# The MLP as a second phase over all tokens, each matrix product in seven half-size ones (Strassen)

## The chip, the cores and the metric

The kernel runs on one core of a Trainium2 chip. The metric is device time in microseconds of one launch. Five engines work side by side, each through its own list of instructions in order: TensorE (PE, with its weight loads as PEld), VectorE (DVE), ScalarE (ACT), GpSimd (POOL), and SyncE (SP), which issues nearly all of the DMAs here. An instruction whose input is not there yet holds up everything behind it on its engine.

## The reference

One layer of a decoder with two kinds of mixer heads: 2048 prompt tokens and 8 x 4 sample tokens, 1024 features, all in fp32.

```python
h = rmsnorm(x, g_mix); proj = h @ w_in              # 1024 x 4624
# RG-LRU: conv, gates, linear recurrence, gelu gate, norm      -> y_lru (1024)
# SSD: conv, silu, 16 heads in chunks of 128, silu gate, norm  -> y_ssd (1024)
x = x + jnp.concatenate([y_lru, y_ssd], axis=-1) @ w_out       # 2048 x 1024
m = rmsnorm(x, g_mlp)
x = x + jnp.square(jax.nn.relu(m @ w_up)) @ w_down             # 1024 x 4096, 4096 x 1024
y = rmsnorm(x, g_final)
```

The states of convolutions and recurrences are outputs too.

## The kernel before

Features lie on the partitions, tokens in the columns. The 2080 tokens are done in three parts of 768, 672 and 640 columns (PARTS), each in two blocks of at most 384 (a PSUM bank): 384 + 384, 384 + 288, 384 + 256. A part runs through all stages before the next one begins: x_phase (load, norm, transpose), dt and group fronts, eight pairs of SSD heads (pair_front, pair_x, pair_mats, pair_back), eight RG-LRU tiles (lru_front, lru_back), the w_out projection in three calls of proj_add, and the MLP. Its last w_down comes after the next part's x_phase in program order; final writes the part's output rows.

An fp32 product is made of three fast ones (mm3, L217): weights and activations are each split into a rounded high half (type fp32r) and the rest, and high by high, low by high and high by low go into one bank (L225 to L227). load_w (L199) brings a weight block of eight 128x128 tiles by one DMA of SP into one of three raw buffers, ScalarE copies it to the high half (L208), and VectorE subtracts for the low half (L214); SHARE and SH1 say which of these subtractions GpSimd takes: those of one w_out call. Loads wait for a raw buffer to come free.

The MLP of a part has four groups of FFQ = 8 feature tiles. up (L787) makes a tile by 24 matmuls for each block, then relu (L800), square (L801), high half (L802) on ScalarE and the low half (L803) on VectorE; proj_add (L413) multiplies by w_down and on VectorE scales by the token's norm (L428) and adds to the residual x (X2 tiles, in SBUF, L429). The norm's square is applied only there, so that up needs no norm. final (L822) turns two tiles of 128 tokens at a time back to rows in four PSUM banks (L837), squares them (L838), takes the reciprocal root by twelve small VectorE operations (rsqrt, L233, and those around it), multiplies (L850) and stores (L853).

The order on every engine is set at build by a scheduler that works from the program's order and its own estimates of when operands are there.

## Time and profile before

| | |
|---|---|
| three runs | 3058.8, 3059.4, 3061.8 us |
| the profiled execution, span of its instructions | 3050.1 us |
| busy PE, DVE, ACT, POOL | 98, 58, 46, 6% |
| instructions PE, DVE, ACT | 19294, 3192, 2424 |
| moved by DMA | 289 MB, 95 GB/s in the mean |
| granted PE clock, mean | 0.993 |

A row of the page's groups reads: line, engine, operation, output from inputs, shapes, count, then busy time in us, mean ns of one, and the engine's idle time before it with what ended it. A window's row gives the busy time of each engine between two moments, with the count of instructions. In time order the MLPs of the three parts lie near 600 to 1040, 1700 to 2050 and 2600 to 3038 us.

### The profile page before, as it was taken

Reading aid. Unit: us, or ns where it says so; the run is one execution under the profiler, and the core shown is the slowest. Engines: PE = TensorE matmul, PEld = TensorE weight load, DVE = VectorE, ACT = ScalarE, POOL = GpSimd, SP = SyncE. Lnnn points to the kernel's source line nnn. Section 1 sums busy time; section 2 is a strip of 40 time slices with the busy share of each in tenths; the row PEclk is TensorE's granted clock in tenths of the full one; section 3 lists DMA queues with packets and bytes.
Section 4 is the critical chain, followed back from the end, with each engine's and each line's share of the span. In section 5 each row is a group of like instructions: output and inputs, shape, how many; then the busy total and the mean of one; then the engine's idle time right before and its main releaser. Section 6 shows DMA issues by size and latency. Waiting matters only on the chain.

```text
span 3050.1 us, 47623 instructions
## 1 busy us (share of the span) xinstructions
PE 2986.8 (98%) x19294; PEld 2914.2 (96%) x19294; DVE 1782.4 (58%) x3192; ACT 1405.8 (46%) x2424; POOL 169.8 (6%) x282
## 2 busy tenths in 40 slices
PE   6999999999999999999989999999999999999998
PEld 5999999999999999999989999999999999999998
DVE  6777677543333457777686433336777677434336
ACT  5543775533241524436855342343554874432333
POOL 1000121000000000001310000000000120000000
PEclk9999999999999999999999999999999999999999
DMA  5332323322222323434233222223343234222224
GB/s 154 95 123 80 98 79 113 98 62 64 64 67 63 98 94 115 143 109 122 85 112 111 73 71 76 70 74 122 112 126 98 80 104 125 84 77 71 76 77 125
DMA packets 447411, 288.85 MB, mean 95 GB/s; under 512 B 23323, under 2 KB 423887, under 8 KB 447190
## 3 DMA queue, kind: packets, MB, share of 16 engines
q1 hardware_dynamic: 446966, 285.52, 31.4%
q8 instruction: 152, 2.49, 0.3%
q0 software_dynamic: 224, 0.27, 0.1%
q14 instruction: 69, 0.57, 0.1%
HBM read 255.95 MB, written 29.79 MB: 94 GB/s over the span
## 4 chain that ended last, share of the span: by engine, by line
PE 78%; DVE 3%; ACT 1%; issue 1%; DMA 1%; DVEq 0%; SPq 0%; ACTq 0%
PE mm L225 24%; PE mm L227 24%; PE mm L226 24%; PE ax L701 1%; PE ax L697 1%; PE ax L673 1%; PE ax L687 1%; PE ax L707 0%; DVE wl L214 0%; ACT wh L208 0%; DMA xT<-xraw 0%; PE ax L613 0%; ACT yt L838 0%; PE ax L757 0%; PE nx L450 0%
## 5 line engine op out<-in xcount | busy, mean ns | idle before, releaser
L225 PE MATMUL mm<-xh,wh 128*128 128x384 f32 (+3 forms) x3696 | 1188.5, 322 | 14.8 <-ACT xh L358 12.7
L227 PE MATMUL mm<-xh,wl 128*128 128x384 f32 (+3 forms) x3696 | 1184.4, 321 | 3.1 <-DVE wl L214 3.1
L226 PE MATMUL mm<-xl,wh 128*128 128x384 f32 (+3 forms) x3696 | 1184.1, 320 | 0.6 <-DVE xl L359 0.5
L208 ACT ACTIVATE wh<-raw 128x1024 fp32r<-128x1024 f32 (+1 forms) x383 | 403.5, 1053 | 1010.3 <-PE mm L226 948.8
L225 PEld LDWEIGHTS mm<-xh,wh 128*128 128x128 f32 (+1 forms) x3696 | 692.1, 187 | 25.6 <-ACT xh L358 13.7
L227 PEld LDWEIGHTS mm<-xh,wl 128*128 128x128 f32 (+1 forms) x3696 | 692.0, 187 | 9.1 <-DVE wl L214 4.4
L226 PEld LDWEIGHTS mm<-xl,wh 128*128 128x128 f32 (+1 forms) x3696 | 692.2, 187 | 5.2 <-DVE xl L359 1.5
L214 DVE TENSOR_TENSOR wl<-raw,wh 128x1024 fp32r<-128x1024 f32 (+1 forms) x371 | 450.9, 1215 | 235.9 <-ACT wh L208 230.3
L225 PE MATMUL mm<-ah,wh 128*128 128x384 f32 (+2 forms) x1536 | 494.2, 322 | 0.0
L227 PE MATMUL mm<-ah,wl 128*128 128x384 f32 (+2 forms) x1536 | 494.0, 322 | 0.0
L226 PE MATMUL mm<-al,wh 128*128 128x384 f32 (+2 forms) x1536 | 493.7, 321 | 0.0
L428 DVE TENSOR_TENSOR mm<-mm,bc 128x384 f32<-128x384 f32 (+2 forms) x336 | 176.0, 525 | 426.8 <-PE mm L227 425.1
L225 PEld LDWEIGHTS mm<-ah,wh 128*128 128x128 f32 x1536 | 289.2, 188 | 0.3
L226 PEld LDWEIGHTS mm<-al,wh 128*128 128x128 f32 x1536 | 289.0, 188 | 0.1
L227 PEld LDWEIGHTS mm<-ah,wl 128*128 128x128 f32 x1536 | 288.9, 188 | 0.1
L803 DVE TENSOR_TENSOR al<-av,ah 128x384 fp32r<-128x384 f32 x192 | 99.7, 519 | 305.0 <-ACT ah L802 304.3
L395 DVE SCALAR_TENSOR_TENSOR u<-xe,prm,u 128x768 f32<-128x768 f32 (+2 forms) x180 | 170.2, 945 | 25.9 <-ACT u L393 23.0
L800 ACT ACTIVATE av<-mm 128x384 f32<-128x384 f32 x192 | 86.4, 450 | 199.2 <-PE mm L227 199.2
L429 DVE TENSOR_TENSOR x<-x,mm 128x384 f32<-128x384 f32 (+2 forms) x336 | 172.2, 513 | 8.7
L225 PE MATMUL mm<-nh,wh 128*128 128x384 f32 (+2 forms) x384 | 128.0, 333 | 10.9 <-DVE x L429 10.7
L226 PE MATMUL mm<-nl,wh 128*128 128x384 f32 (+2 forms) x384 | 126.1, 328 | 0.0
L227 PE MATMUL mm<-nh,wl 128*128 128x384 f32 (+2 forms) x384 | 126.0, 328 | 0.0
(266 smaller groups left out, 2891.5 us busy)
## 6 DMA issues: line engine op xcount, KB each, us to landing
raw<-in_w_in_dram SPq DMA_DIRECT2D x108, 512.0 KB
raw<-in_w_down_dram SPq DMA_DIRECT2D x104, 512.0 KB
raw<-in_w_up_dram SPq DMA_DIRECT2D x96, 512.0 KB
raw<-in_w_out_dram SPq DMA_DIRECT2D x72, 512.0 KB
m<-cum SPq DMA_DIRECT2D x32, 320.0 KB
xt<-in_x_prompt_dram SPq DMA_DIRECT2D x13, 512.0 KB
xT<-xraw SPq DMA_DIRECT2D x32, 192.0 KB
m<-cum SPq DMA_DIRECT2D x16, 384.0 KB
```

Of the source, the lines that this page charges most:

```text
L208: S.activation(h, raw, AF.Copy)
L214: e.tensor_tensor(out=lo, in0=raw, in1=h.bitcast(F32), op=ALU.subtract)
L225: T.matmul(ps[:m, :n], h[:, k, :m], xh[:, c0:c0 + n], start=k == 0, stop=False)
L226: T.matmul(ps[:m, :n], h[:, k, :m], xl[:, c0:c0 + n], start=False, stop=False)
L227: T.matmul(ps[:m, :n], lo[:, k, :m], xh[:, c0:c0 + n], start=False, stop=k == nk - 1)
L395: V.scalar_tensor_tensor(out=u[:, :W], in0=xe[:, k:k + W], scalar=pc(wn, k * nt + j), in1=u[:, :W], op0=ALU.mult, op1=ALU.add)
L428: V.tensor_mul(ps[:, :n], ps[:, :n], bc[:, c0:c0 + n])
L429: V.tensor_add(P.X2[o][:, c0:c0 + n], P.X2[o][:, c0:c0 + n], ps[:, :n])
L673: T.matmul(ps[:, c * Q:c * Q + Q], R.bk[:, (a + c) * Q:(a + c + 1) * Q], xdd[:, (a + c) * Q:(a + c + 1) * Q], start=True, stop=True)
L687: T.matmul(ps, xds[:, 1], R.bex[:NS, 512 * i:512 * i + 512], start=True, stop=True)
L800: S.activation(v[:, :n], ps[:, :n], AF.Relu)
L803: V.tensor_sub(lo[:, c0:c0 + n], v[:, :n], h[:, c0:c0 + n].bitcast(F32))
```

## The change

The MLP leaves the parts. First all three parts go through the mixer stages and w_out. After each block of w_out, residual_out writes the normalised input of the MLP (with its gain) and the residual to DRAM (mn_d, x2_d). Then all mixer pools are closed and mlp() runs over all 2080 tokens, in three groups of 2 x 348 or 2 x 346 columns.

There each product is taken as a 2 x 2 product of blocks: input features in two halves, output features in two halves, tokens in two halves. Seven products of sums of blocks take the place of eight (the Winograd form, 4 sums of weight blocks, 4 of activation blocks, 7 of results). Some results are summed in PSUM, by a second product into the same bank (start=False). The seven weight operands, with high and low halves, do not depend on the tokens: they are made once, in 64 jobs that stand between the steps of the mixers. A job has four stages (load four blocks; four sums and the high half; store the high half and subtract; store the low half), and each call of tick in the mixers puts 1.0, 1.4 or 1.6 of these stages in program order at its place. They go to DRAM; the MLP loads its weights from there as finished halves, for each token group again, by 240 DMAs of up to 512 KB. jt and jh, the jobs' tiles, have one buffer each; to make room in SBUF raw has two buffers, not three, and there are 20 slots, not 22. GpSimd's share of the low halves is gone.

up makes two columns of feature tiles by seven products of 12 matmuls, twice a group of features (eight groups); the sums, relu and squares give four tiles, from which operands() makes the seven operands in halves for down. down makes four pairs of output tiles by seven products of 6 matmuls each; sums go to u (the part that three results share) or straight to x2. final takes a tile of 128 tokens at a time.

```diff
-NW = 22
-FFQ = 8
+NW = 20
 XG = 3
 KEEP = 7
-SHARE, SH1 = 0, 1
 NK = 5
+MLP = [(0, 348), (696, 346), (1388, 346)]
+MH, FQ = 348, 4
+NTOK = SEQ + NS
+TP, TL, TO = 1.4, 1.6, 1.0
...
-        raw = room("raw", F32, 3)
+        raw = room("raw", F32, 2)
-        e = V
-        if share:
-            gwn[0] += 1
-            e = G if gwn[0] % share == 0 else V
-        e.tensor_tensor(out=lo, in0=raw, in1=h.bitcast(F32), op=ALU.subtract)
+        V.tensor_tensor(out=lo, in0=raw, in1=h.bitcast(F32), op=ALU.subtract)
...
+            if tick:
+                tick(P, TO)
...
+    def mlp():
+        mp = ctx.enter_context(tc.tile_pool(name="mp", bufs=1, reuse_waits="tile"))
+        sf = ctx.enter_context(tc.tile_pool(name="sf", bufs=3, reuse_waits="tile"))
+        ps8 = ctx.enter_context(tc.tile_pool(name="ps8", bufs=6, space=PSUM))
+        psf = ctx.enter_context(tc.tile_pool(name="psf", bufs=2, space=PSUM))
...
+        def weights(src, op, m):
+            w = mp.tile([128, 2, 512], F32R, tag="mw", name="mw", bufs=6)
+            nc.sync.dma_start(w[:, :, :m].bitcast(F32), src[:, op])
+            return w
+        def product(ps, w, ops, n, start):
+            nk = len(ops)
+            for k, (xh, xl) in enumerate(ops):
+                c = slice(128 * k, 128 * k + 128)
+                for i, (wi, x) in enumerate(((0, xh), (0, xl), (1, xh))):
+                    T.matmul(ps[:, :n], w[:, wi, c], x[:, :n], start=start and k == 0 and i == 0,
+                             stop=k == nk - 1 and i == 2, skip_group_check=not start)
+        def halves(t, n, tag, bufs):
+            h = mp.tile([128, MH], F32R, tag=tag, name=tag + "h", bufs=bufs)
+            lo = mp.tile([128, MH], F32R, tag=tag, name=tag + "l", bufs=bufs)
+            S.activation(h[:, :n], t[:, :n], AF.Copy)
+            V.tensor_sub(lo[:, :n], t[:, :n], h[:, :n].bitcast(F32))
+            return h, lo
+        def operands(b, n, tag, bufs):
+            b11, b12, b21, b22 = b
+            t1, t2, t3, t4 = (tmp(f"t{i}") for i in range(4))
+            V.tensor_sub(t1[:, :n], b12[:, :n], b11[:, :n])
+            V.tensor_sub(t2[:, :n], b22[:, :n], t1[:, :n])
+            V.tensor_sub(t3[:, :n], b22[:, :n], b12[:, :n])
+            V.tensor_sub(t4[:, :n], b21[:, :n], t2[:, :n])
+            return [halves(t, n, tag, bufs) for t in (b11, t2, t1, t3, b21, b22, t4)]
+        def front(c0, n):
...
+        def up(q, u, mh, n):
+            src = up_d[2 * q + u]
+            x, y, z, w = bank(), bank(), bank(), bank()
+            product(x, weights(src, 0, 512), mh[0], n, True)
+            p1 = tmp("p1")
+            S.activation(p1[:, :n], x[:, :n], AF.Copy)
+            product(y, weights(src, 1, 512), mh[1], n, True)
+            v = tmp("v")
+            V.tensor_add(v[:, :n], p1[:, :n], y[:, :n])
+            product(z, weights(src, 2, 512), mh[2], n, True)
+            p5 = tmp("p5")
+            S.activation(p5[:, :n], z[:, :n], AF.Copy)
+            product(w, weights(src, 3, 512), mh[3], n, True)
+            c22 = tmp("c22")
+            V.tensor_add(c22[:, :n], v[:, :n], w[:, :n])
+            V.tensor_add(c22[:, :n], c22[:, :n], p5[:, :n])
+            product(x, weights(src, 4, 512), mh[4], n, False)
+            c11 = tmp("c11")
+            S.activation(c11[:, :n], x[:, :n], AF.Relu)
+            product(z, weights(src, 5, 512), mh[5], n, False)
+            c12 = tmp("c12")
+            V.tensor_add(c12[:, :n], v[:, :n], z[:, :n])
+            product(w, weights(src, 6, 512), mh[6], n, False)
+            c21 = tmp("c21")
+            V.tensor_add(c21[:, :n], v[:, :n], w[:, :n])
+            for c in (c22, c12, c21):
+                S.activation(c[:, :n], c[:, :n], AF.Relu)
+            for c in (c11, c12, c21, c22):
+                S.activation(c[:, :n], c[:, :n], AF.Square)
+            return operands((c11, c12, c21, c22), n, "ah", 29)
+        def down(q, act, x2, us, n, steps):
+            for g in range(4):
+                if steps:
+                    steps.pop(0)()
+                src = dn_d[4 * q + g]
+                hi, lo = x2[g], x2[g + 4]
+                c11, c12, c21, c22 = hi[:, :n], hi[:, n:2 * n], lo[:, :n], lo[:, n:2 * n]
+                def add(c, ps):
+                    V.tensor_add(c, c, ps[:, :n])
+                x, y, z, w = bank(), bank(), bank(), bank()
+                ws = {}
+                def prod(i, ps, start):
+                    if i % 2 == 0:
+                        t = mp.tile([128, 2, 512], F32R, tag="mw", name="mw", bufs=6)
+                        m = min(2, 7 - i)
+                        tv = t.rearrange("p a (b c) -> p (a b c)", c=256)[:, :m * 512]
+                        nc.sync.dma_start(tv.bitcast(F32).rearrange("p (o c) -> p o c", c=512),
+                                          src[:, i:i + m].rearrange("p o h c -> p o (h c)"))
+                        ws[0] = t.rearrange("p a (b c) -> p a b c", c=256)
+                    product(ps, ws[0][:, i % 2], [a[i] for a in act], n, start)
+                u = us[g][:, :n]
+                prod(0, x, True)
+                if q == 0:
+                    S.activation(u, x[:, :n], AF.Copy)
+                else:
+                    add(u, x)
+                prod(1, y, True)
+                add(u, y)
+                prod(2, z, True)
+                add(c22, z)
+                prod(3, w, True)
+                add(c22, w)
+                prod(4, x, False)
+                add(c11, x)
+                prod(5, z, False)
+                add(c12, z)
+                prod(6, w, False)
+                add(c21, w)
+                if q == NQ - 1:
+                    for c in (c12, c21, c22):
+                        V.tensor_add(c, c, u)
+        def final(c0, n, x2):
...
+                    ps = psf.tile([128, 512], F32, tag="fx", name="fx")
...
+                        T.transpose(ps[:m, 128 * k:128 * k + 128], x2[4 * hf + k][:, o:o + m], ident)
...
+                    S.activation(yt[:m], ps[:m], AF.Square, accum_out=s2[:m, hf:hf + 1])
...
+                rsqrt(rs[:m], ss[:m], 1, sf)
...
+                    V.scalar_tensor_tensor(out=yts[hf][:m], in0=pss[hf][:m], scalar=rs[:m, 0:1],
+                                           in1=gfb[:m, 512 * hf:512 * hf + 512], op0=ALU.mult, op1=ALU.mult)
...
+        mh, steps = front(*MLP[0])
+        for f in steps:
+            f()
+        prev = None
+        for i, (c0, n) in enumerate(MLP):
+            us = [mp.tile([128, MH], F32, tag="u", name="u", bufs=4) for _ in range(4)]
+            x2 = None
+            for q in range(NQ):
+                act = [up(q, u, mh, n) for u in range(2)]
+                if prev:
+                    final(*prev)
+                    prev = None
+                if x2 is None:
+                    x2 = []
+                    for o in range(KD):
+                        t = mp.tile([128, 2 * MH], F32, tag="x2", name="x2", bufs=8)
+                        nc.sync.dma_start(t[:, :2 * n], x2_d[128 * o:128 * o + 128, c0:c0 + 2 * n])
+                        x2.append(t)
+                steps = []
+                if q == NQ - 1 and i + 1 < len(MLP):
+                    mh, steps = front(*MLP[i + 1])
+                    steps.pop(0)()
+                down(q, act, x2, us, n, steps)
+            prev = (c0, n, x2)
+        final(*prev)
...
+    def job_load(j):
+        src, ld, r0, dr_, cols, _ = jobs[j]
+        t = jt[j] = wp.tile([128, 7, 256], F32, tag="jt", name="jt", bufs=1)
+        for i, at in ((0, (0, 4)), (1, (3, 6))):
+            for k in range(2):
+                nc.sync.dma_start(t[:, at[k]].rearrange("p (k n) -> p k n", n=128),
+                                  dap(src, (r0 + dr_ * k) * ld + cols[i], [[ld, 128], [128 * ld, 2], [1, 128]]))
+    def job_sums(j):
+        t = jt[j]
+        V.tensor_add(t[:, 2], t[:, 3], t[:, 6])
+        V.tensor_sub(t[:, 3], t[:, 0], t[:, 3])
+        V.tensor_sub(t[:, 1], t[:, 2], t[:, 0])
+        V.tensor_sub(t[:, 5], t[:, 4], t[:, 1])
+        h = jh[j] = wp.tile([128, 7, 256], F32R, tag="jh", name="jh", bufs=1)
+        S.activation(h, t, AF.Copy)
+    def job_lower(j):
+        nc.sync.dma_start(jobs[j][5][:, :, 0], jh[j].bitcast(F32))
+        V.tensor_tensor(out=jt[j].bitcast(F32R), in0=jt[j], in1=jh[j].bitcast(F32), op=ALU.subtract)
+    def job_store(j):
+        nc.sync.dma_start(jobs[j][5][:, :, 1], jt[j])
+        del jt[j], jh[j]
+    stages = (job_load, job_sums, job_lower, job_store)
+    def tick(P, w):
+        clock[1] += w
+        while clock[1] >= 1 and clock[0] < 4 * len(jobs):
+            clock[1] -= 1
+            stages[clock[0] % 4](clock[0] // 4)
+            clock[0] += 1
...
             xx = pair_x(P, pr, fr[0])
+            tick(P, TP)
             nx = ahead()
+            tick(P, TP)
             if pr == 4:
                 load_x2(P)
                 proj_add(P, w_out, 8, n0, bc0)
             ms_ = pair_mats(P, R, pr)
+            tick(P, TP)
             y, acc = pair_back(P, R, pr, fr, acc, ms_, xx)
+            tick(P, TP)
...
+        def residual_out(b):
+            rstd_rows(P, rstd_sums(P, accs[b], D, EPS, [P.groups[b]]), [P.groups[b]], AF.Copy, P.bc2)
             for k, t in enumerate(P.X2):
-                split(t[:, c0:c0 + n], pc("g_m", k), mh[b][k], n)
-                accs[b] = squares(accs.get(b), t, c0, n)
...
         for b in range(lastb + 1):
-            proj_add(P, w_out, 0, nl, bcl, [b])
+            proj_add(P, w_out, 0, nl, bcl, [b], tick=tick)
+            sums(b)
             if b < lastb:
-                mlp_in(b)
-        nq = FF // 128 // FFQ
-        for q in range(nq):
-            act = up(P, q, mh, (lambda: mlp_in(lastb)) if q == 0 else None)
-            if q == 0:
-                mlp_norm()
-                carried_out(P)
-            if q < nq - 1:
-                proj_add(P, w_down, q * FFQ, act, P.bc2)
+                residual_out(b)
+        carried_out(P)
         if not P.last:
             x_phase(parts[P.i + 1])
-            proj_add(P, w_down, (nq - 1) * FFQ, act, P.bc2)
-            for g in P.groups:
-                final(P, g)
-        else:
-            for b, g in enumerate(P.groups):
-                proj_add(P, w_down, (nq - 1) * FFQ, act, P.bc2, [b])
-                final(P, g)
+        residual_out(lastb)
+    tick(P, 999)
+    mix.close()
+    mlp()
```

How the order moves at three places that matter. First VectorE, where a group of features goes from up to down. Before, in the MLP of the second part (al is the low half, x the residual, bc the norm's row):

```order
L803 TENSOR_TENSOR al<-av,ah 128x384
L214 TENSOR_TENSOR wl<-raw,wh 128x1024
L803 TENSOR_TENSOR al<-av,ah 128x288
L428 TENSOR_TENSOR mm<-mm,bc_16025 128x384
L429 TENSOR_TENSOR x_11939<-x_11939,mm 128x384
```

After, in the second token group (c are up's four results, t the sums of them, ahh and ahl the halves, u the shared part of down's results, mb a PSUM bank):

```order
L905 TENSOR_TENSOR c_23493<-v,mb 128x346
L908 TENSOR_TENSOR c_23509<-v,mb 128x346
L830 TENSOR_TENSOR t_23518<-c_23493,c_23477 128x346
L924 TENSOR_TENSOR u<-u,mb 128x346
L831 TENSOR_TENSOR t_23519<-c_23460,t_23518 128x346
L832 TENSOR_TENSOR t_23520<-c_23460,c_23493 128x346
L833 TENSOR_TENSOR t_23521<-c_23509,t_23519 128x346
L823 TENSOR_TENSOR ahl<-t_23519,ahh 128x346
L823 TENSOR_TENSOR ahl<-t_23518,ahh 128x346
```

Before, the low half of one tile stood between those of others and the first sum of w_down came after the last. Now the sum of down's first product (L924) stands ahead of the sums and low halves that down's later products need.

Second TensorE, where the last w_down of the first part ends, before (x are the residual tiles, 16 such transposes make two tiles of tokens):

```order
L226 MATMUL mm<-al,wh 128x384
L227 MATMUL mm<-ah,wl 128x384
L837 MATMUL ax<-ident,x_2136 128x128
L837 MATMUL ax<-ident,x_2138 128x128
```

After, where the second token group's first down begins (ident marks a transpose of final, mb a product):

```order
L816 MATMUL mb<-ahh,mw 128x346
L975 MATMUL fx<-ident,x_18064 128x128
L975 MATMUL fx<-ident,x_18066 128x128
L975 MATMUL fx<-ident,x_18068 128x128
L975 MATMUL fx<-ident,x_18070 128x128
L816 MATMUL mb<-ahh,mw 128x346
L816 MATMUL mb<-ahl,mw 128x346
```

The transposes of final stand among the products of the next token group, and those of tile after tile in one list. Third, SP's DMAs at the end of the mixers of the last part, before:

```order
L206 DMA raw<-in_w_out_dram 128x8x128 x13
L206 DMA raw<-in_w_up_dram 128x8x128 x8
L206 DMA raw<-in_w_down_dram 128x8x128 x5
L866 DMA out_dram<-st 3x512 x5
```

After:

```order
L1030 DMA out_dram<-st 3x512 x5
L1044 DMA out_dram<-st 8x128
L1051 DMA out_dram<-st 128x4x128 x2
L1238 DMA mn_d<-mn 128x256 x8
L796 DMA gfb<-in_g_final_dram 128x1024
L847 DMA mb<-mn_d 128x348 x16
L807 DMA mw<-up_139 128x1024 x7
L807 DMA mw<-up_140 128x1024 x4
```

Weights for the MLP followed those of w_out directly; now eight stores of the last block's normalised input and sixteen loads of the first token group's stand between.

194 lines of the change are left out of this document (107 added, 87 removed).

## The prediction

> **What bounds the kernel now.** I read the busy shares, the chain that ended last, then the groups that make up the MLP.
>
> ```profile
> span 3050.1 us, 47623 instructions
> PE 2986.8 (98%) x19294; PEld 2914.2 (96%) x19294; DVE 1782.4 (58%) x3192; ACT 1405.8 (46%) x2424; POOL 169.8 (6%) x282
> PE   6999999999999999999989999999999999999998
> PE 78%; DVE 3%; ACT 1%; issue 1%; DMA 1%; DVEq 0%; SPq 0%; ACTq 0%
> L225 PE MATMUL mm<-ah,wh 128*128 128x384 f32 (+2 forms) x1536 | 494.2, 322 | 0.0
> ```
>
> TensorE is the bound: busy 98% of the span, 78% of the chain, and idle only in the first slice. So fewer matmul columns are worth their time, and anything that makes TensorE wait costs in full. The third row is w_down: 1536 matmuls for one of the three half-products; w_up has as many (8 k-tiles x 32 features x 6 blocks), so the MLP is 2 x 3 x 1536 = 9216 matmuls.
>
> The windows inside the MLP of each part (first three) and in the mixers (the others) show what stands beside them. Columns: window and length, then busy time of PE, PE loads, VectorE, ScalarE, GpSimd, granted clock, DMA share, GB/s.
>
> ```profile
> 600.00:1040.00 440.00, 440.00 (x2535) 439.57 (x2534) 152.11 (x244) 142.03 (x230) 0.00 (x0) 1.00 0.22 64
> 1760.00:2040.00 280.00, 280.00 (x1832) 280.00 (x1831) 102.09 (x147) 100.01 (x168) 0.00 (x0) 1.00 0.25 72
> 2600.00:2980.00 380.00, 380.00 (x2600) 379.46 (x2599) 144.85 (x228) 136.37 (x234) 0.00 (x0) 1.00 0.27 77
> 40.00:560.00 520.00, 512.61 (x3109) 498.11 (x3108) 389.18 (x629) 285.90 (x463) 50.29 (x69) 0.99 0.33 100
> 1120.00:1640.00 520.00, 510.13 (x3452) 481.86 (x3451) 399.30 (x794) 286.36 (x501) 64.06 (x128) 1.00 0.40 118
> 2130.00:2580.00 450.00, 441.46 (x3086) 427.54 (x3085) 346.45 (x631) 263.29 (x442) 49.59 (x69) 1.00 0.36 108
> 2130.00:2370.00 240.00, 238.88 (x1719) 229.59 (x1718) 188.75 (x387) 118.35 (x234) 15.17 (x36) 1.00 0.38 113
> 2480.00:2530.00 50.00, 44.64 (x284) 41.88 (x283) 43.81 (x78) 30.26 (x47) 11.09 (x7) 0.97 0.36 112
> 1540.00:1580.00 40.00, 33.95 (x212) 31.52 (x211) 37.58 (x75) 21.23 (x32) 6.72 (x7) 0.96 0.33 106
> ```
>
> In the MLP TensorE never stops and VectorE is busy only 35 to 38%. In the mixers VectorE is already busy 75 to 77%, and TensorE 98%. The last three rows are finer: at 79% of VectorE TensorE idles 0.5%; where VectorE reaches 88 and 94%, TensorE idles 11 and 15%.
>
> **The change, part by part.** The sum is made against the profiled span, 3050.1 us; the median of the runs, 3059.4, is 9.3 more, which I add at the end.
>
> *Fewer matmuls.* One matmul takes 440.00/2535 = 173.6 ns where blocks are 384 wide, 152.8 at a mean width of 336, 146.2 at 320: about 0.43 ns a column, 157.8 at 347. Before: 3072 x (173.6 + 152.8 + 146.2) = 1452 us. After, 8 groups of features x 3 groups of tokens x (2 x 84 + 4 x 42) = 8064 matmuls of 346 or 348 columns: 1272 us. **-180 us.** This is all that the change can win.
>
> *The jobs in the mixers.* 64 of them: four VectorE sums of 128x256, a ScalarE copy and a VectorE difference of 128x1792, four loads and two stores. Their nearest rows:
>
> ```profile
> L214 DVE TENSOR_TENSOR wl<-raw,wh 128x1024 fp32r<-128x1024 f32 (+1 forms) x371 | 450.9, 1215 | 235.9 <-ACT wh L208 230.3
> L803 DVE TENSOR_TENSOR al<-av,ah 128x384 fp32r<-128x384 f32 x192 | 99.7, 519 | 305.0 <-ACT ah L802 304.3
> L208 ACT ACTIVATE wh<-raw 128x1024 fp32r<-128x1024 f32 (+1 forms) x383 | 403.5, 1053 | 1010.3 <-PE mm L226 948.8
> L802 ACT ACTIVATE ah<-av 128x384 fp32r<-128x384 f32 x192 | 94.9, 494 | 6.0
> L214 POOL TENSOR_TENSOR wl<-raw,wh 128x1024 fp32r<-128x1024 f32 x12 | 30.3, 2526 | 27.2 <-ACT wh L208 22.4 <-DVE ul L735 4.8
> SPq L206 <- DVE wl L214: 1875.2, 297, 18.5
> ```
>
> A VectorE difference takes 519 ns at a mean of 347 columns and 1215 at 1024: 1.03 ns a column and 160 fixed. So a sum is 0.42 us, the difference 2.0, a job 4 x 0.42 + 2.0 = 3.7 us; 64 make 237 us. The 12 differences that GpSimd had (30.3 us there) come to VectorE at 1.2: 15 more. Over the 1490 us of mixer windows this is 17 points: VectorE goes from 76 to **93%**. ScalarE gets 64 x 1.7 = 109 us, to 63%: no bound. The bounds of what this does to TensorE: nothing (the 79% window), and the 12% between the 88 and 94% windows: 180 us. I take 5%, **+75 us**: 93% is nearer to the bad windows, but those also hold the norms' own chains at group and part ends, in which TensorE waits whatever VectorE has to do. A thing that favours the upper end: the six DMAs of a job go through SP's queue among the weight loads, and a store waits there for the job's copy or difference. Behind it wait the raw weights of the next projection, with two buffers instead of three; SP already waits 1875 us for VectorE to free them.
>
> *From up to down, 24 times.* Before, another tile's columns covered the relu chain. Now the second up's last product ends in a chain that all seven operands share. Counted from the end of that product, at half a microsecond each (519, 494, and the next two rows):
>
> ```profile
> L800 ACT ACTIVATE av<-mm 128x384 f32<-128x384 f32 x192 | 86.4, 450 | 199.2 <-PE mm L227 199.2
> L429 DVE TENSOR_TENSOR x<-x,mm 128x384 f32<-128x384 f32 (+2 forms) x336 | 172.2, 513 | 8.7
> ```
>
> VectorE does the last sum (L908), t1 (L830), then in its queue the down's first u (L924), which waits 0.95 us for six matmuls, then t2, t3, t4 and only then t2's low half: near 3.5 us. TensorE has nine matmuls that need none of it, 1.42 us, and takes a high half at 2.4. It stands some 1.9 us; 22 times (the other two fall in the next term) **+42**. Below: 0, if the down's first product and ScalarE's copies come earlier than I count; above, 60.
>
> *Between token groups, twice.* Final takes one tile of 128 tokens after another, since its two banks hold one tile, and the next down adds to x2, which is loaded over the tiles that final still reads. The last tiles of before show the price:
>
> ```profile
> 3038.41 2.02 PE L837 MATMUL ax<-ident,x 128*128 128x128 f32 x16
> 3039.05 0.60 ACT L838 ACTIVATE yt<-ax 128x512 f32<-128x512 f32 x1 [5.16 <-PE ax L837]
> 3041.79 0.16 DVE L841 TENSOR_TENSOR ssq<-s 128x1 f32<-128x1 f32 x1 [1.00 <-ACT yt L838]
> 3043.97 0.16 DVE L245 SCALAR_TENSOR_TENSOR rs<-nq,rs 128x2 f32<-128x2 f32 x1
> 3044.23 2.73 DVE L850 SCALAR_TENSOR_TENSOR yt<-ax,rs,gfb 128x512 f32<-128x512 f32 x4
> 3045.01 2.31 SPq L853 DMA_DIRECT2D out_dram<-yt  x4
> 3038.50:3050.10 11.60, 1.93 (x17) 1.56 (x15) 5.69 (x19) 2.53 (x8) 0.00 (x0) 0.74 0.24 90
> ```
>
> Eight transposes 1.0, a square 0.6, twelve small operations 2.34 (3041.79 to 3044.13), two of L850 1.37: 5.3 us a tile, six tiles 32. The first hides in the chain above, and five products of the down (4.7 us) can run before its first sum on x2 is needed: 22 each, **+44** (20 to 60). The next group's operands also fall on VectorE in the last down: 44 differences and 28 sums, 72 x 0.51 = 37 us beside 168 x 157.8 ns = 26.5; half of the difference is hidden since products take operands in order: 5 each, **+10** (0 to 20).
>
> *From the mixers to the MLP, once.* New in the path: at the durations above squares 3, statistics and reciprocal root 2.5, row broadcast 1.3, eight products by the gain and norm 4, a store and a load through DRAM (from the last output's issue, near 3047, to the end at 3050.1: 3 each, so 6), the first halves 2, and VectorE, slower than TensorE on the first up (22 us of differences beside 13.3), 6: **+25** (12 to 40). x_phase of the next part has lost the last w_down that covered it; the last w_out blocks cover most: **+10** over two parts (0, and twice the start, where the first slice of the page has TensorE at 6 tenths of 76 us, 30 idle). *The tail:* the last sums 3, six tiles 32, output 3 are 38 us after the last product instead of 11.6: **+26** (15 to 30). Half clock after these gaps (a row below): **+5**.
>
> Sum: -180 + 75 + 42 + 44 + 10 + 25 + 10 + 26 + 5 = **+57 us**: span 3107, time 3116.
>
> *The weight stream* I cost at nothing. The MLP reads 240 blocks for each token group, 117 MB, three times: 352 MB in 1272 us, 277 GB/s, where the page's busiest slice moves 154 and the start:
>
> ```profile
> GB/s 154 95 123 80 98 79 113 98 62 64 64 67 63 98 94 115 143 109 122 85 112 111 73 71 76 70 74 122 112 126 98 80 104 125 84 77 71 76 77 125
> 7.00:12.00 5.00, 1.98 (x10) 1.99 (x11) 0.36 (x4) 2.75 (x9) 0.00 (x0) 1.00 1.03 408
> 487.50:494.00 6.50, 6.50 (x24) 6.50 (x24) 5.24 (x16) 0.07 (x1) 0.00 (x0) 0.50 0.69 246
> ```
>
> 408 GB/s over 5 us, so the engines can; the cover is six buffers ahead of TensorE. The Trainium skill (DMA: Bandwidth & Descriptors, the section on the anatomy of one DMA) fits a transfer as about 2.0 us fixed plus its bytes at 436 GB/s; an estimate from it is 3.2 us for a 512 KB block, against 12 x 157.8 ns = 1.9 us of TensorE for its product. One load at a time would by that add 1.3 us for each of 624 full blocks, some 800 us; six in flight hide it. The same page's rule (Rule under the measured bandwidths) asks for 1 MiB or more in one DMA, twice these blocks, and speaks against the change; the row of 408 GB/s was made of blocks of 512 KB and smaller, so I go by the row. The last row is the clock at half for 6.5 us, which the +5 above rests on.
>
> **The rivals.** A: *VectorE's idle time takes it.* The mixer loses 5 instead of 75, and with VectorE free in the MLP the in-order waits come out near their lower ends (25 for 42, 35 for 44): 57 - 70 - 17 - 9 = -39, time 3020. For it: TensorE at 99.5% beside VectorE at 79%, spaced ticks, jobs that nothing in the mixer waits for. Against it: 93% as a mean means stretches above 100. In between, only the mixer 60 better, it is 3056: no change. B: *the mixers become VectorE's.* TensorE idles there 12%, as between the two narrow windows: 180 instead of 75, time 3221; it decides where VectorE's mean passes the 88% of the window at 2480. C: *the stream doesn't flow*: at the 154 GB/s of the busiest slice 352 MB take 2286 us, 1014 more than the matmuls: 4130. The 408 GB/s row speaks against it, and the DMA engines' share of 1.03 there says that this was their top. That the change doesn't do what it says, less work on TensorE, I exclude: the matmuls are counted.
>
> **How the numbers follow.** What a measurement of this kernel can tell from no change is about 0.2%, 6 us. My forecast, slower by the sum, 0.50; A 0.28 (faster); the case in between 0.07 (same); B 0.11; C 0.04. So faster 0.28, same 0.07, slower 0.65. Most likely time 3116, its own range 3070 to 3180 (the ends of the mixer, up-to-down and group terms that are likely together). The range of 8 in 10 reaches down into A and up to short of B: 3010 to 3195.
>
> **What would show it.** In the profile after: x8064 matmuls of L816 at about 158 ns apart in the middle of a down; VectorE above 90% in mixer windows with TensorE at 92 to 94% there; idle time of TensorE before down's products released by the low halves of L823, 1 to 3 us at a time, 22 times; two gaps of some 20 us with final's small VectorE operations in them; about 38 us after the last L816. I am wrong if the mixer windows keep TensorE at 98% (then A), or if TensorE's waits name the weights' DMA (C). A single mixer term of over 150 us would be B.

## The result and the profile after

The changed kernel takes 3188.7 us (median of four runs, 3186.8 to 3198.0); beside it the kernel before took 3059.8 (3058.8 to 3061.8). The ratio is 1.0433, with a 95% interval of 1.0412 to 1.0454: slower, as forecast, but by 129 us where 57 were forecast.

The page of the changed kernel: span, busy time of the engines, then TensorE's busy tenths and granted clock in 40 slices, the traffic, and the chain of work that ended last.

```profile
span 3185.0 us, 49175 instructions
PE 2922.6 (92%) x18150; PEld 2812.0 (88%) x18150; DVE 2207.3 (69%) x4423; ACT 1407.6 (44%) x2580; POOL 158.8 (5%) x270
PE   7999999899999878998986999999799998699996
PEclk9999999899999988999997999999899999799997
GB/s 190 171 227 172 183 195 205 251 187 198 194 187 172 167 268 217 164 207 157 224 171 220 304 270 281 268 284 270 233 274 280 270 283 259 220 269 276 267 279 150
PE 47%; DVE 5%; DMA 5%; ACT 2%; issue 1%; SPq 0%; DVEq 0%; POOL 0%; ACTq 0%
```

TensorE was busy 98% of the time and is now busy 92%. The idle time went from 63.3 us (3050.1 - 2986.8) to 262.4. The slices with a 6, 7 or 8 are in the first 22 (the mixers) and at the three places where a token group ends. From the 23rd slice to the last but one, 220 to 304 GB/s are moved, nearly all of it weights of the MLP.

Windows by stage, the three mixers of before and then, of after, the three mixers (the third with the way into the MLP), the MLP and the tail. The columns are those of the prediction's windows.

```profile
27.30:573.00 545.70, 534.57 (x3223) 515.62 (x3224) 408.79 (x673) 302.37 (x500) 50.48 (x70) 0.98 0.34 103
1120.70:1639.00 518.30, 508.43 (x3440) 480.16 (x3439) 397.63 (x791) 284.66 (x497) 64.06 (x128) 1.00 0.40 119
2122.00:2582.00 460.00, 450.92 (x3154) 434.56 (x3153) 354.65 (x656) 268.27 (x457) 49.59 (x69) 1.00 0.36 109
```

```profile
26.20:591.50 565.30, 542.10 (x3252) 520.15 (x3252) 477.08 (x822) 337.21 (x528) 49.96 (x66) 0.98 0.65 200
591.50:1201.60 610.10, 555.51 (x3480) 509.11 (x3481) 482.67 (x938) 332.04 (x556) 60.92 (x126) 0.93 0.66 198
1201.60:1756.80 555.20, 481.95 (x3173) 454.76 (x3172) 442.25 (x812) 306.36 (x499) 45.50 (x67) 0.93 0.64 195
1756.80:3146.10 1389.30, 1325.35 (x8162) 1312.97 (x8163) 778.57 (x1742) 412.55 (x949) 0.00 (x0) 0.97 0.81 268
3146.10:3185.00 38.90, 10.91 (x49) 8.43 (x46) 20.83 (x87) 8.24 (x24) 0.00 (x0) 0.57 0.20 74
```

| stage | before, us | after, us | difference |
|---|---|---|---|
| to the first projection | 27.3 | 26.2 | -1 |
| mixers | 1524.0 | 1730.6 | +207 |
| MLP | 1487.3 | 1389.3 | -98 |
| tail | 11.5 | 38.9 | +27 |

The MLP of before is what lies between its mixers; besides its 9216 matmuls (1452 us) it held 35 us of other things, the next part's x_phase and final among them.

The mixers lost more than twice what the MLP won. Two causes show in these rows: TensorE's idle time in the mixers (151 us against 30), and the clock, which was 0.98 to 1.00 and is now 0.93 in two of the three. Two matmuls of 384 columns start 174 ns apart at full clock before (175 after), and 320 at half in both (the median over each trace's pairs). TensorE was busy at half clock for 25 us of the execution before and for 194 now. Work done there takes 320/174 of its time, so 0.456 of it is lost: 11 us before, 89 now. So the span of 134.9 us more is: idle +199; busy -64, and that is -170 of fewer matmuls, +77 of the clock, and 29 that I cannot assign (waits that the modelled ends of the matmuls hide may be among them). Of the 77, 50 lie in the mixers (135.4 us of busy time at half clock for 24.8), 22 in the MLP and 4 in the tail.

The waits of TensorE, in us, times and the longest:

```profile
PE fx L975 <- DVE yt L985: 56.7, 13, 6.4
PE mb L816 <- DMA mw<-up: 25.5, 3, 20.6
PE mm L225 <- ACT wh L212: 23.3, 11, 7.7
PE mm L227 <- DVE wl L214: 16.9, 21, 1.7
PE mm L225 <- ACT xh L359: 15.5, 4, 9.5
```

The first row is final, tile after tile (the two gaps and the tail). The second is the way into the MLP. The third and fourth are weights of the mixers whose halves came late; in the kernel before, TensorE waited 3.1 us in all for low halves, by this row of its page:

```profile
L227 PE MATMUL mm<-xh,wl 128*128 128x384 f32 (+3 forms) x3696 | 1184.4, 321 | 3.1 <-DVE wl L214 3.1
```

After the first group of features, the MLP of the first token group runs without a stop. In the whole MLP TensorE stands idle for 64 us, 58 of them in the two gaps between token groups, and of down's waits for the high or low half of an operand one row is left, 1.4 us, once:

```profile
1900.00:2160.00 260.00, 260.00 (x1635) 259.41 (x1634) 139.67 (x293) 71.07 (x161) 0.00 (x0) 1.00 0.83 276
PE mb L816 <- ACT ahh L822: 1.4, 1, 1.4
```

1635 matmuls in 260 us are 159.0 ns each, so the 8064 take 1282 us.

### The profile page after: what moved, and what is told of

Read it like the earlier page. It is cut to its first block, busy times and chain, and to the rows that moved or that the text cites. A ratio compares the mean times of both kernels' runs of the same rounds, so it can differ in the third digit from the quotient of the medians.

```text
span 3185.0 us, 49175 instructions
## 1 busy us (share of the span) xinstructions
PE 2922.6 (92%) x18150; PEld 2812.0 (88%) x18150; DVE 2207.3 (69%) x4423; ACT 1407.6 (44%) x2580; POOL 158.8 (5%) x270
## 4 chain that ended last, share of the span: by engine, by line
PE 47%; DVE 5%; DMA 5%; ACT 2%; issue 1%; SPq 0%; DVEq 0%; POOL 0%; ACTq 0%
PE mb L816 39%; PE mm L227 2%; PE mm L225 2%; PE mm L226 2%; DMA out_dram<-yt 1%; DMA mb<-mn_d 1%; DMA m<-cum 1%; DMA mw<-up 1%; DVE wl L214 0%; DMA mw<-dn 0%; DMA raw<-in_w_out_dram 0%; DVE yt L985 0%; DVE jt L1091 0%; PE ax L704 0%; DMA dn<-jt 0%
## 5 line engine op out<-in xcount | busy, mean ns | idle before, releaser
L225 PE MATMUL mm<-xh,wh 128*128 128x384 f32 (+3 forms) x2160 | 715.8, 332 | 49.4 <-ACT wh L212 22.0
L227 PE MATMUL mm<-xh,wl 128*128 128x384 f32 (+3 forms) x2160 | 711.9, 331 | 13.4 <-DVE wl L214 13.3
L226 PE MATMUL mm<-xl,wh 128*128 128x384 f32 (+3 forms) x2160 | 710.0, 329 | 1.5 <-DVE xl L360 0.8
L816 PE MATMUL mb<-ahh,mw 128*128 128x346 f32 (+1 forms) x2688 | 659.6, 326 | 18.9 <-DVE nt L242 7.7
L816 PE MATMUL mb<-mhh,mw 128*128 128x346 f32 (+1 forms) x2688 | 650.8, 322 | 25.5 <-DMA mw<-up 25.5
L816 PEld LDWEIGHTS mb<-ahh,mw 128*128 128x128 f32 x2688 | 476.0, 192 | 25.7 <-DVE nt L242 8.7
L816 PEld LDWEIGHTS mb<-mhh,mw 128*128 128x128 f32 x2688 | 475.0, 191 | 26.4 <-issue 21.0
L816 PE MATMUL mb<-ahl,mw 128*128 128x346 f32 (+1 forms) x1344 | 436.1, 325 | 0.1
L816 PE MATMUL mb<-mhl,mw 128*128 128x346 f32 (+1 forms) x1344 | 436.1, 325 | 0.0
L227 PEld LDWEIGHTS mm<-xh,wl 128*128 128x128 f32 (+1 forms) x2160 | 410.9, 190 | 26.6 <-DVE wl L214 20.4
L924 DVE TENSOR_TENSOR x<-x,mb 128x346 f32<-128x346 f32 (+1 forms) x480 | 244.3, 514 | 151.5 <-PE mb L816 148.3
L214 DVE TENSOR_TENSOR wl<-raw,wh 128x1024 fp32r<-128x1024 f32 (+1 forms) x183 | 220.4, 1205 | 43.9 <-ACT wh L212 42.4
```

The lines of the kernel that those rows point to most:

```text
L214: V.tensor_tensor(out=lo, in0=raw, in1=h.bitcast(F32), op=ALU.subtract)
L225: T.matmul(ps[:m, :n], h[:, k, :m], xh[:, c0:c0 + n], start=k == 0, stop=False)
L226: T.matmul(ps[:m, :n], h[:, k, :m], xl[:, c0:c0 + n], start=False, stop=False)
L227: T.matmul(ps[:m, :n], lo[:, k, :m], xh[:, c0:c0 + n], start=False, stop=k == nk - 1)
L816: T.matmul(ps[:, :n], w[:, wi, c], x[:, :n], start=start and k == 0 and i == 0, stop=k == nk - 1 and i == 2, skip_group_check=not start)
L924: V.tensor_add(c, c, ps[:, :n])
```

## The experiments

Twelve kernels ran, in three groups of four; the kernel before, run beside each group, took 3056.3, 3050.4 and 3059.2 us. Each is one time and one profile, and the scheduler puts each kernel's instructions in an order of its own: the first part's mixers took 565 us in the changed kernel and 579 with the DMAs of the jobs alone, which is less work, so single stages are not read closer than some 15 us. The rivals at the start were V, VectorE is crowded by the jobs' sums; D, the jobs' DMAs hold up SP's queue and the weights; and B, the part borders and the smaller buffers cost it, not the jobs.

### Without jobs, and with one half of a job each

Without jobs:

```diff
-    up_d = [dr.tile([128, 7, 2, 512], F32, name=f"up{j}") for j in range(2 * NQ)]
+    up_d = [dr.tile([128, 7, 2, 512], F32, name="up0")] * (2 * NQ)
...
-            stages[clock[0] % 4](clock[0] // 4)
+            if clock[0] < 12:
+                stages[clock[0] % 4](clock[0] // 4)
```

> Only three of the 64 weight jobs run, all in the first part; the MLP reads one pair of their outputs again and again, so its output is not the reference's, but its loads, products and order are kept. The mixers of the second and third part, 610 and 555 us with the jobs (519 and 461 before), show what the jobs cost. Theory V (VectorE is crowded by the jobs' sums) and theory D (the jobs' DMAs hold up SP's queue and the weight loads) both expect the mixers back near 530 and 490 and about 3050 in all. Theory B (the growth comes from the part borders, the two raw buffers and the lost GpSimd share, not from the jobs) expects them to stay above 580 and 530, 3130 in all or more.

The DMAs alone:

```diff
     def job_sums(j):
-        t = jt[j]
-        V.tensor_add(t[:, 2], t[:, 3], t[:, 6])
...
+        pass
     def job_lower(j):
-        nc.sync.dma_start(jobs[j][5][:, :, 0], jh[j].bitcast(F32))
-        V.tensor_tensor(out=jt[j].bitcast(F32R), in0=jt[j], in1=jh[j].bitcast(F32), op=ALU.subtract)
+        nc.sync.dma_start(jobs[j][5][:, :, 0], jt[j])
```

> All 64 jobs load and store as before, but no engine computes anything for them: what is stored is what was loaded (the sums and halves are left out, so the MLP's output is not the reference's). Theory V: as without jobs, within 20 us, about 3060. Theory D: as the changed kernel, 3170 to 3190. If both count, between, near 3110.

The sums alone:

```diff
     def job_load(j):
         src, ld, r0, dr_, cols, _ = jobs[j]
+        t = jt[j] = jtp
+        if j > 2:
+            return
...
     def job_lower(j):
-        nc.sync.dma_start(jobs[j][5][:, :, 0], jh[j].bitcast(F32))
+        if j < 3:
+            nc.sync.dma_start(jobs[j][5][:, :, 0], jh[j].bitcast(F32))
```

> All 64 jobs compute (four sums, the high half, the low half), but only three load and store: the others work on a tile that stays, so the MLP reads one pair of outputs and its output is not the reference's. Theory V: VectorE as busy as in the changed kernel, 3160 to 3190. Theory D: as without jobs, about 3060.

Measured: 3063.5 us without jobs, 3126.3 with the DMAs alone, 3147.3 with the sums alone. Mixers and the way into the MLP in one window, of the changed kernel, then without jobs, DMAs alone, sums alone:

```profile
26.20:1756.80 1730.60, 1579.57 (x9902) 1484.02 (x9903) 1402.00 (x2570) 975.60 (x1581) 156.39 (x259) 0.94 0.65 197
```

```profile
26.30:1636.60 1610.30, 1537.06 (x9902) 1458.56 (x9903) 1215.19 (x2265) 879.48 (x1520) 139.72 (x259) 0.97 0.40 123
```

```profile
26.20:1693.40 1667.20, 1564.66 (x9902) 1478.82 (x9902) 1205.33 (x2248) 876.32 (x1517) 138.35 (x259) 0.95 0.67 205
```

```profile
26.00:1714.20 1688.20, 1566.12 (x9902) 1479.29 (x9902) 1394.52 (x2569) 976.09 (x1581) 171.11 (x259) 0.95 0.39 117
```

The jobs (61 of the 64, as three still run) cost 120 us of the mixers (1730.6 - 1610.3): idle 78, lost to the clock 33, the rest busy. Neither V nor D is the whole of it: the sums alone cost 78, the DMAs alone 57; that the two add up to 15 more than both together is within what single runs can tell. And B holds a part: without the jobs the kernel is no faster than before, with mixers 86 us longer.

D as it was put, with the weight loads held up, is not what the DMAs alone did. TensorE's waits for weights stay as they were without jobs (7.3 us for low halves, then 6.0); what is longer is ScalarE's wait for m, a tile of the SSD heads that comes through the same queue, and behind it TensorE's for what is made of m, a row that the run without jobs does not have. The DMAs alone, then without jobs:

```profile
ACT m L644 <- DMA m<-cum: 41.7, 17, 7.6
PE ax L704 <- DVE m L646: 11.4, 5, 4.9
PE mm L227 <- DVE wl L214: 7.3, 9, 1.7
```

```profile
ACT m L644 <- DMA m<-cum: 7.0, 7, 2.3
PE mm L227 <- DVE wl L214: 6.0, 7, 1.7
```

TensorE's wait for the high halves of weights, 23.3 us in the changed kernel, is 1.8 with the DMAs alone and 3.1 with the sums alone: it is long only where both run. Whether the loads come late through SP's order or through the traffic, these rows don't say.

### Half the jobs, and the long operations cut

```diff
-TP, TL, TO = 1.4, 1.6, 1.0
+TP, TL, TO = 0.7, 0.8, 0.5
...
-    up_d = [dr.tile([128, 7, 2, 512], F32, name=f"up{j}") for j in range(2 * NQ)]
+    up_d = [dr.tile([128, 7, 2, 512], F32, name=f"up{j}") for j in range(NQ)] * 2
...
-    for q in range(NQ):
+    for q in range(NQ // 2):
```

> The changed kernel with 32 jobs instead of 64 at half the density; the MLP's second half of features reads the operands of the first half, so its output is not the reference's. All 64 jobs cost 125 us against none. If the cost goes with the load (each job delays something), 32 cost about 60: 3125. If it is a queue that fills as VectorE nears its limit (92% with all, about 84% with half), 32 cost 15 to 40: 3080 to 3105.

Measured: 3111.2 us. The mixers:

```profile
26.20:1678.20 1652.00, 1551.45 (x9902) 1468.66 (x9902) 1300.46 (x2408) 924.96 (x1549) 149.63 (x259) 0.96 0.53 161
```

32 jobs cost 42 us there where 64 cost 120. It lies between the two cases, nearer to a queue that fills up: the second 32 jobs cost 78. With 15 us of doubt on each, that the second half costs more than the first is likely, its size is not.

```diff
-        S.activation(h, t, AF.Copy)
+        for a in range(0, 7, 2):
+            S.activation(h[:, a:min(a + 2, 7)], t[:, a:min(a + 2, 7)], AF.Copy)
...
-        V.tensor_tensor(out=jt[j].bitcast(F32R), in0=jt[j], in1=jh[j].bitcast(F32), op=ALU.subtract)
+        for a in range(0, 7, 2):
+            t = jt[j][:, a:min(a + 2, 7)]
+            V.tensor_tensor(out=t.bitcast(F32R), in0=t, in1=jh[j][:, a:min(a + 2, 7)].bitcast(F32), op=ALU.subtract)
```

> The changed kernel with a job's long operations cut in four: ScalarE's copy and VectorE's difference of 1792 columns become three of 512 and one of 256. If long operations hurt (2.0 us of VectorE and 1.7 us of ScalarE in which a short one on the way to TensorE must wait), the mixers gain some of the 84 us that the sums alone cost: 3150 to 3175. If only the amount of VectorE's work counts, the 0.5 us more a job (0.16 us for each extra start) make it 5 to 20 us more: 3190 to 3210.

Measured: 3217.3 us, 29 more than the changed kernel and more than either case gave. So the long operations are not the cause. That the amount of work is, is not shown by this: VectorE was busy 8 us more in the mixers (1409.5 for 1402.0) and ScalarE 25, and they took 28 us longer.

### The work given to GpSimd, and the queue given to ScalarE

```diff
-        V.tensor_add(t[:, 2], t[:, 3], t[:, 6])
+        G.tensor_add(t[:, 2], t[:, 3], t[:, 6])
...
-        V.tensor_tensor(out=jt[j].bitcast(F32R), in0=jt[j], in1=jh[j].bitcast(F32), op=ALU.subtract)
+        G.tensor_tensor(out=jt[j].bitcast(F32R), in0=jt[j], in1=jh[j].bitcast(F32), op=ALU.subtract)
```

> The jobs' four sums and the low half go to GpSimd, everything else is kept. By the rate of GpSimd's 128x1024 difference before (2.5 us) a job takes some 7.5 us there, 480 us in all, on an engine that is busy 159. Theory V: VectorE's busy share in the mixers falls by 14 points and the time to about 3080. Theory D: 3170 to 3190, since the DMAs are the same and the stores wait longer.

Measured: 3359.7 us, 171 more than the changed kernel and more than either case gave. The mixers:

```profile
26.30:1923.30 1897.00, 1626.94 (x9902) 1521.66 (x9903) 1389.66 (x2249) 975.94 (x1581) 648.05 (x579) 0.92 0.59 180
```

VectorE was given 321 instructions less (2249 for 2570) and is busy just as long: 1389.7 us against 1402.0 with the jobs and 1215.2 without. Its own instructions became slower. Two of its groups, first of the changed kernel, then of this one:

```profile
L214 DVE TENSOR_TENSOR wl<-raw,wh 128x1024 fp32r<-128x1024 f32 (+1 forms) x183 | 220.4, 1205 | 43.9 <-ACT wh L212 42.4 <-DMA y<-ecum 0.9
L396 DVE SCALAR_TENSOR_TENSOR u<-xe,prm,u 128x768 f32<-128x768 f32 (+2 forms) x180 | 169.7, 943 | 12.6 <-ACT u L394 10.6
```

```profile
L214 DVE TENSOR_TENSOR wl<-raw,wh 128x1024 fp32r<-128x1024 f32 (+1 forms) x183 | 236.8, 1296 | 33.1 <-ACT wh L212 32.2
L396 DVE SCALAR_TENSOR_TENSOR u<-xe,prm,u 128x768 f32<-128x768 f32 (+2 forms) x180 | 190.1, 1056 | 39.9 <-ACT u L394 32.9 <-issue 3.7
```

So this run could not take VectorE's load away, and it does not decide between V and D.

```diff
-                nc.sync.dma_start(t[:, at[k]].rearrange("p (k n) -> p k n", n=128),
+                nc.scalar.dma_start(t[:, at[k]].rearrange("p (k n) -> p k n", n=128),
...
-        nc.sync.dma_start(jobs[j][5][:, :, 0], jh[j].bitcast(F32))
+        nc.scalar.dma_start(jobs[j][5][:, :, 0], jh[j].bitcast(F32))
...
-        nc.sync.dma_start(jobs[j][5][:, :, 1], jt[j])
+        nc.scalar.dma_start(jobs[j][5][:, :, 1], jt[j])
```

> The changed kernel, but the jobs' loads and stores are issued by ScalarE and not by SP. With the DMAs alone the changed kernel took 63 us more than without jobs. If that is SP's queue (a store that waits there for its job holds up the raw weights behind it), most of the 63 goes: about 3130 to 3150. If it is the traffic itself (150 MB more beside the weight loads), or if ScalarE pays for the waits in its turn, 3170 to 3200.

Measured: 3322.4 us, more than any case gave. TensorE's wait for high halves of weights, which ScalarE makes, is larger (23.3 in the changed kernel), and that for low halves too:

```profile
PE mm L225 <- ACT wh L212: 40.8, 18, 6.9
PE mm L227 <- DVE wl L214: 36.3, 32, 5.4
```

That fits ScalarE paying for the jobs' waits in its turn, and the low halves come later too; but the two rows are 37 us more, and the mixers are 127 longer (1857.2 for 1730.6: 81 idle, 41 lost to the clock). That SP's queue was a part of D is neither shown nor excluded by this.

### The borders

Three raw buffers, 22 slots and GpSimd's share back, no jobs (the lines for that and for the weights that are stored instead are left out here):

```diff
-        raw = room("raw", F32, 2)
+        raw = room("raw", F32, 3)
...
-NW = 20
+NW = 22
...
-        V.tensor_tensor(out=lo, in0=raw, in1=h.bitcast(F32), op=ALU.subtract)
+        e.tensor_tensor(out=lo, in0=raw, in1=h.bitcast(F32), op=ALU.subtract)
```

> No jobs at all (the MLP's weights are a few halves of other weight blocks stored once in the first part and read again and again, so its output is not the reference's), and what was taken away for the jobs is given back: three raw buffers, 22 slots, GpSimd's share of the low halves. Without jobs but with the smaller buffers the mixers took 554, 554 and 503 us against 546, 519 and 461 before. If the buffers and GpSimd's share made these 84 us, the mixers come back to within 15 us of before plus the way into the MLP (some 35): about 3010 in all. If the borders make them (the next part's x_phase without a last w_down beside it, the residual's way out and in), the mixers stay near 550 and 500: 3050 to 3063.

Measured: 3062.3 us; the first MLP matmul at 1634.5 (1636.6 with the smaller buffers). Without jobs, the buffers and GpSimd's share cost nothing that can be seen; whether two raw buffers make the jobs dearer, no run tried. By elimination, the 86 us are the borders: 43 of them are idle time of TensorE (73.2 us for 30.1) and 17 the clock. No run took the MLP as a second phase with eight products, so this price is not measured by itself. A good third of the 86 was in the MLP's windows before (35 us of x_phase and others); 29 are the way into the MLP (no w_out or MLP matmul from 1727.8 to 1756.8).

### The gaps between token groups, and the way in

```diff
-                act = [up(q, u, mh, n) for u in range(2)]
-                if prev:
-                    final(*prev)
-                    prev = None
+                fin = final(*prev) if prev else iter(())
+                prev = None
+                act = [up(q, u, mh, n, fin) for u in range(2)]
+                for _ in fin:
+                    pass
...
             product(y, weights(src, 1, 512), mh[1], n, True)
+            next(fin, None)
```

> The changed kernel, but final's tiles of the last token group stand between the products of the next group's first two ups, one tile after every second product, and no longer in a block after them. If the two gaps between token groups (94 and 96 us with 59 us of work) come from final's tiles one after another, they shrink to under 70 each: 45 to 60 us less in all, about 3130 to 3145. If they come from the next group's operands or from x2's loads, under 15 us less.

Measured: 3153.4 us. The two gaps, of the changed kernel and then with the tiles spread:

```profile
2176.10:2269.60 93.50, 65.06 (x379) 61.37 (x378) 64.51 (x186) 33.35 (x84) 0.00 (x0) 0.82 0.65 219
2650.60:2746.10 95.50, 65.82 (x378) 62.51 (x377) 63.68 (x184) 33.39 (x84) 0.00 (x0) 0.82 0.63 211
```

```profile
2176.40:2257.00 80.60, 62.74 (x379) 59.34 (x378) 63.08 (x186) 33.18 (x84) 0.00 (x0) 0.92 0.75 256
2634.70:2714.60 79.90, 62.88 (x379) 59.22 (x377) 63.12 (x186) 33.31 (x84) 0.00 (x0) 0.94 0.78 256
```

13 and 16 us less in the gaps, 33 less over the whole MLP (1355.8 us for 1389.3), not the 45 to 60 expected, and they stay at 80 us. Final's tiles in a row are about a third of what the gaps lose (some 42 us each over the time of their matmuls); the rest (18 us of idle in each) names several waits of 2 to 5 us and no single cause.

```diff
-        carried_out(P)
         if not P.last:
             x_phase(parts[P.i + 1])
         residual_out(lastb)
+        carried_out(P)
...
+        early.extend([weights(up_d[0], k, 512) for k in range(6)])
         mh, steps = front(*MLP[0])
```

> The changed kernel with the spread final (35 us less when it ran alone), the first six weight loads of the MLP ahead of the sixteen loads of its input, and the states' way out behind the residual's. The way from the last w_out matmul to the first of the MLP took 29 us, of which 6 are the states' transposes and copies ahead of the norm's row and 5 the wait for weights behind the sixteen loads: so 8 to 12 us less than the spread final alone, 3140 to 3146. If the chain of stores and loads through DRAM sets it alone, no difference to it: 3150 to 3156.

Measured: 3141.6 us, 12 less than the spread final alone, as the first case gave, but not for its reason. The way in hardly got shorter: from the last w_out matmul at 1713.0 to the MLP's first at 1740.9 it is 28 us for 29. With the weights there first, TensorE waits for the first high half, and ScalarE, which makes it, for the input that comes through DRAM:

```profile
PE mb L820 <- ACT mhh L826: 15.7, 2, 14.8
ACT mhh L826 <- DMA mb<-mn_d: 26.2, 4, 21.3
```

So the chain through DRAM sets the way in. The gain lies in the mixers ahead of it, which came out 16 us shorter (1714.7 to the MLP's first matmul, for 1730.6) in another order; that is little more than the 15 us by which such stages differ anyway. It is the fastest version of this design that ran and computes everything, still 2.7% behind the kernel before.

```diff
+            dummy = bank()
...
+                for _ in range(16):
+                    T.matmul(dummy[:, :MLP[-1][1]], mh[0][0][0][:, :128], mh[0][0][0][:, :MLP[-1][1]], start=True, stop=True)
```

> The changed kernel with extra matmuls that nobody reads: 16 of 346 columns after the transposes of each of final's tiles, into a PSUM bank of their own, so that TensorE has some 2.5 us of work in each 5.3 us tile at the group gaps. In the changed kernel's trace the clock is at half for 33 and 35 us in the two gaps and for some 7 us behind each. If the clock is a cause of its own (it falls when TensorE was used too little in the 3.4 us before, and costs as much again as the wait), the extra matmuls keep it full there and the work behind the gaps runs at its full rate: 0 to 15 us less in spite of 90 more matmuls each (14 us at full clock, laid into waits). If half clock only comes along with waits and costs nothing by itself, the extra matmuls are pure cost or hidden: 0 to 25 us more.

Measured: 3198.9 us, 10 more than the changed kernel and so in the range of the second case, but 8 of these lie in the mixers, which were not touched (1738.6 for 1730.6). The MLP took 1393.0 us, with 192 matmuls more than the changed kernel's 1389.3:

```profile
1764.90:3157.90 1393.00, 1349.90 (x8354) 1339.08 (x8355) 780.19 (x1744) 412.87 (x949) 0.00 (x0) 0.98 0.80 267
```

The clock was at half for 49 us of it instead of 94, but TensorE's own work at half clock fell only from 49 to 37, which is 5 us of lost time: there was little to win here. The 192 matmuls, 30 us of work, cost 4. Undecided.

### From up to down

The same matmuls in number and shape, but as the weights keep their places, each weight meets the other up's operand, so the MLP's output is not the reference's.

```diff
-                    product(ps, ws[0][:, i % 2], [a[i] for a in act], n, start)
+                    product(ps, ws[0][:, i % 2], [a[i] for a in act[::-1]], n, start)
```

> The changed kernel, but each product of down takes the operand of the second up first and that of the first up second; the same matmuls. If the wait from up to down that was forecast (1.9 us, 22 times) is real but covered by matmuls on the first up's operands that the scheduler puts ahead, it must appear here: 2 to 4 us before each of 24 downs, 45 to 100 us more, about 3240 to 3280. If the chain is simply short, nothing changes: 3185 to 3195.

Measured: 3249.3 us. The wait that was missing is there, and the MLP took 1450.0 us for 1389.3:

```profile
PE fx L975 <- DVE yt L985: 49.9, 13, 6.2
PE mb L816 <- ACT ahh L822: 35.7, 23, 1.6
1758.50:3208.50 1450.00, 1359.77 (x8162) 1335.46 (x8163) 787.89 (x1741) 412.23 (x949) 0.00 (x0) 0.96 0.77 257
```

These are 23 waits of 1.55 us, 36 us together; but the MLP is 61 us longer. 21 stretches of half clock begin in it instead of 6, and TensorE's busy time at half clock rises from 49 to 92 us, which loses 20 more. TensorE's idle time in the MLP rose by 26 us only (90 for 64), since other waits, final's above all, got shorter; some 15 of the 61 stay unassigned. So a wait of about a microsecond and a half cost about half as much again through the clock here. No other kernel shows it as cleanly, because the work is the same and only the order of the operands was changed.

## Why the prediction was right and wrong

| term of the forecast | forecast | measured |
|---|---|---|
| fewer matmuls | -180 | -170 (8064 at 159.0 ns for 157.8) |
| jobs in the mixers | +75 | +120 |
| x_phase uncovered, and from the mixers to the MLP | +10, +25 | +51 (86 less the 35 that lay in the MLP's windows) |
| from up to down | +42 | 1.4, once |
| between token groups, and their operands | +44, +10 | +84 (the stretches of 93.5 and 95.5 us, less 330 matmuls each) |
| the rest of the MLP | 0 | +23 (1389.3 - 1282 - 84) |
| tail and start | +26 | +26 (27 - 1) |
| half clock after the gaps | +5 | +77 wherever the clock fell, contained in the rows above |

**What failed is the term "Half clock after these gaps (a row below): +5".** The idle time was forecast about right in the sum: 75 + 42 + 44 + 10 + 25 + 10 + 26 = 232 us, and 199 were measured. That is partly luck: the 42 from up to down did not come, and the gaps and the borders took more than they were given. But I took each wait as its bare length, and looked for half clock only behind the gaps. The clock lost 89 us against 11: 50 more in the mixers, where the sum has nothing for it, 22 in the MLP, 11 of these in the two gaps, and 4 in the tail. It was to be had from the rows of before: those two windows in which TensorE idles 11 and 15% have a granted clock of 0.97 and 0.96, and the stretch at 487.5 had TensorE busy for all of 6.5 us at half clock. I took that for a detail of five microseconds, in place of a price on every wait.

*The jobs.* The load was right: VectorE's busy time in the mixers rose by 241 us (1402.0 for 1161.1; 237 and 15 were forecast), to 92% of TensorE's work in them (1518 us: its busy time less what the clock lost). But the mixers got longer, so the sign "VectorE above 90% in mixer windows" is not in the rows: it is 84, 79 and 80% of the three windows, beside 96, 91 and 87% of TensorE. TensorE's idle time was right too, 78 us for the 75 forecast; the 120 are these, the clock (33) and 9 more. The 75 was a choice between 0 and 180, made for VectorE's load, so that it came out so close is luck: the "thing that favours the upper end", the DMAs on SP's queue, is real in size (57 us alone), and its mechanism is not shown. My bound from the two narrow windows, 180, was not reached.

*From up to down.* The chain was counted right: t2's low half at 3.5 us. The cover was counted wrong: "nine matmuls that need none of it, 1.42 us". In the order on TensorE, in 21 of the 24 downs, 17 of down's matmuls stand before the first that takes the high half of the second up's t2, and 22 before the one that takes its low half, 3.5 us: just enough. The scheduler had put the first up's operands of three more products ahead. The reversed kernel shows that this cover is what hides the chain.

*Between groups.* 22 + 5 for each were forecast, 42 measured. The spread final shows that final's row of tiles is some 15 of these; what remains has several causes, left open.

*The way in.* 29 us for the 25; the 22 left of the borders' 51, for which x_phase had 10, are not taken apart further.

*The weight stream* flows: 276 GB/s over 260 us with TensorE never idle, from blocks of 512 KB and less. The Trainium skill's rule for blocks of 1 MiB or more (DMA: Bandwidth & Descriptors, under the measured bandwidths) did not bear here: with six blocks ahead, the smaller ones brought all that TensorE took. The fit that the prediction takes from the Trainium skill (the section on the anatomy of one DMA, under the same title) is stated there for DMAs that GpSimd issues; these are SP's, and no run here shows the 2.0 us. TensorE's waits that name weights of the MLP are 31 us in all, 20.6 of them one wait on the way in. *The rivals:* A fell (the mixers lost 207 us, not 5); B's condition, VectorE above 88%, holds by TensorE's work (92%) and not by the time of the mixers (81%), and the jobs cost two thirds of its price, 120 us of 180; C fell.

## What to carry to other kernels

Where TensorE is the bound, price a wait at its length and once more for the clock: here 199 us of idle time took 77 more in lost clock, and in one variant waits of 1.55 us, spread out, cost half as much again. Before moving work "into the idle time" of another engine, take the busy share of that engine after the move. VectorE's busy time over TensorE's work in the mixers was 81% without jobs, 86 with half of them and 92 with all: the first half cost 42 us, the second 78. A saving of an eighth of the matmuls in half of the time is 170 us; the borders, gaps and the preparation of its operands were 305.

## What the runs showed of the hardware

**The clock gate counts use in windows of 3.41 us.** All stretches of half clock in these traces are multiples of 3.413 us long, but for the last of each, in which the trace ends. I cut the 14 traces into such windows, in step with the clock's records, and counted what followed a window at full clock. Where TensorE was used for less than 0.4 of it, the next window was at half in 277 of 312; from 0.4 to 0.5 in 81 of 100; from 0.5 to 0.6 in 65 of 162; at 0.6 and above in 38 of 11,245. Back from half it needs more: the next window was full in 405 of 457 after a use of 0.9 or more, in 38 of 70 at 0.8 to 0.9, and below that in 4 of 624. So it is not the long waits alone: about 2 us of idle time inside one window were mostly enough, and the next 3.4 us ran at half, which loses 1.6 if TensorE is busy in them. The Trainium skill (TensorE: Matmul & The Clock Gate, the section on what's actually happening) puts the drop after an idle window of about 3.4 us; the length of the window agrees, but windows that were half used dropped too.

**GpSimd's work beside VectorE slowed VectorE.** With GpSimd busy for 648 us of the mixers instead of 156, VectorE's 128x1024 difference took 1296 ns for 1205, the 128x768 multiply-add 1056 for 943, and its busy time without the jobs rose from 1215 to 1390 us. VectorE's busy time hardly fell although the jobs' work had left it. Within that one run, the 48 such differences that had GpSimd busy beside them for over half of their time took 1523 ns in the mean, and the 114 that had it idle 1219; the sums of the residual (L432), which read one of their two inputs from PSUM, took 549 and 551.
